# A hybrid decoder block on one core: unnormalised x + mixer split into three parts straight from its PSUM banks, and the RMS factor applied per expert place

## The chip, the cores and the metric

The kernel runs on 1 core of one Trainium2 chip. The metric is the device time of one execution in microseconds. Three runs of the kernel before gave 624.11, 624.51 and 628.24 us (median 624.51). The engines are called as the profile calls them: PE (matmul), PEld (PE's weight loads), DVE (vector), ACT (activation), POOL (GpSimd) and SP, which here only issues DMAs.

## The reference, cut to what matters

```python
# x: (1, 256, 1024) float32; 256 tokens, 1024 features; 4 groups x 8 experts, top 2 of one group per token
x = x + hybrid_mixer(rmsnorm(x, norm_mix_g), ...)          # mLSTM heads and S5 groups, then @ w_out
t = rmsnorm(x, norm_ffn_g)                                 # x * rsqrt(mean(x*x) + EPS) * g
g_logits = t @ rg_w + rg_b;  e_logits = t @ re_w + re_b    # choose a group, then two of its experts
for e in range(32):
    ye = (silu(t @ w_gate[e]) * (t @ w_up[e])) @ w_down[e]  # 1024 -> 512 -> 1024, all float32
    y = y + combine[:, e:e + 1] * ye
return rmsnorm(x + y, norm_final_g)
```

The 32 experts' weights are 192 blocks of 1 MiB, and each is read once.

## The kernel before, in words

**Tiling.** The 256 tokens are two blocks (b = 0, 1) of 128 partitions. The kernel has three stages. The mixer ends with `outs` (L797), which adds mixer @ w_out to x in four PSUM banks `WB` = 0, 1, 5, 7, one for each token block b and half q of the features. A prologue (L1015 to L1071) routes the tokens. A loop over 16 pairs of experts (L1083) follows, and then a tail.

**The prologue.** `residual` copies each bank to `x1` (a 1 MiB buffer, half 5). `squares` makes the sums from which POOL computes `r2`, the factor rsqrt(mean + EPS) of each token. `transpose1` and `logits` give the router's products. `choose` and `rank` are chains of small DVE instructions: which two experts a token takes (`msk`), and which of the 64 places of the expert it gets (`rk`). `rank` needs one small matmul (L899) between `choose` and its own DVE step (L901). `warm` is filler matmuls of the identity. `first` (L937) then writes a float32 one-hot matrix, times r2, and `gather_first` (L943) multiplies `x1` by it: the tokens of the first pair, sorted by place, in float32. `gains` (L950, DVE) multiplies by g2 into `xg`, the moving side of the expert products.

After the gather, DVE and ACT work out the mixing weights (`weights`, L909 to L917), and L1061/L1062 the largest number of tokens of an expert, in PSUM bank `UB` = 4. `parts_of_x` (L919) then makes x * r2 in a scratch buffer (half 22) and splits it into three bf16 parts `xp` whose sum is the float32 value. The gathers of all later pairs (L967) read these parts with bf16 one-hots `oh`: 48 matmuls, in pair 0 for pair 1 and in every odd pair up to 13 for the next two pairs.

**A pair.** The gate products (16 matmuls in bank `GB` = 2), Silu on ACT (L1096), the up products (16 in bank 4), act * up on DVE (L1103), four PE transposes (L1117), and the scatter operand: two transposes of the one-hot weights into columns 0 to 255 of bank 4 (L982), reduced and compared on DVE (L984, L985). Then comes the gather, if the pair has one, and the down products (16). All these matmuls are L994. The scatter of the pair before (L1009) lies between gate, up and transposes.

**What sets the order.** The schedule is manual: each engine runs its instructions in the order in which the program writes them, and the framework puts semaphore waits where two engines touch the same data. All PSUM work goes through one tile of eight banks.

**The weight queue.** `fetch(n)` issues the DMAs of the first n weight blocks, in order, on SP (L147). The blocks rotate through 23 buffers in the order `RO`; a DMA waits until its buffer's former user is done, and everything behind it on SP waits too. Blocks 21 and 22 (counted from 0) go into half 5, which is `x1`, and half 22, the scratch of `parts_of_x`. Block 23 reuses the buffer of block 0 and is free when half of pair 0's gate products are done.

Of the kernel before, what the change touches and what calls it, by code (L numbers as in the profile page):

```python
# [20 lines left out]
D = 1024  # L21
# [51 lines left out]
def tile_hymba(ctx, tc, x, norm_mix_g, w_in, conv_w, conv_b, i_bias, f_bias, mlstm_norm_g,  # L73
# [37 lines left out]
    oh = cuts(cst.bitcast(BF16), (2, 4, 64), start=2 * 1176)[0]  # L111
    ru = pool.tile([P, 2, 2, 8], U32, name="ru")
# [5 lines left out]
    RO = (14, 16, 18, 11, 10, 4, 19, 15, 7, 17, 20, 21, 12, 8, 1, 6, 0, 2, 3, 9, 13, 5, 22)  # L118
# [696 lines left out]
    fetch(14)  # L815
# [19 lines left out]
    fetch(16)  # L835
# [3 lines left out]
    fetch(18)  # L839
# [12 lines left out]
    def squares(b, q, e):  # L852
        cs = slice(512 * q, 512 * q + 512)
        if e is V:
            STT(sqs[:, cs], x1[:, b, cs], 1.0 / D, x1[:, b, cs], OP.mult, OP.mult, accum_out=sh[:, b, q:q + 1])
        else:
            ACT(sqs[:, cs], x1[:, b, cs], AF.Square, scale=1.0 / 32, accum_out=sh[:, b, q:q + 1])
# [39 lines left out]
    def rank(b):  # L897
# [5 lines left out]
        for e in range(2):  # L903
            first(b, e)
            yield
# [13 lines left out]
    def parts_of_x(b):  # L919

        t, r = xn[:, b], xp[:, :, b]
        ACT(t, x1[:, b], AF.Copy, scale=r2[:, b:b + 1])
        A.copy(r[:, 0], t)
        yield
        TT(t, t, r[:, 0], OP.subtract)
        A.copy(r[:, 1], t)
        yield
        TT(r[:, 2], t, r[:, 1], OP.subtract)

    xg, act, aT, ow, oh32 = cuts(mw, (8, 256), 512, (4, 128), (2, 2, 64), (2, 2, 64))
# [3 lines left out]
    def first(b, e):  # L936
        TS(oh32[:, b, e], places, rk[:, b, e:e + 1], r2[:, b:b + 1], OP.is_equal, OP.mult)  # L937

    def gather_first(q, bs=(0, 1)):
# [12 lines left out]
    def onehots(e0, es):  # L952

        for b in range(2):
# [80 lines left out]
    run(outs(7, 3, (1,), (1,)))  # L1035
    residual(1, 1)
# [3 lines left out]
    squares(1, 1, A)  # L1040
    warm(3, DN[0])
# [3 lines left out]
    run(rank0)  # L1045
    rank1, ch = rank(1), choose(1)
    next(ch)
    gather_first(0, (0,))
    gather_first(1, (0,))
    MM(PS[:, LB[1], 64:96], ones, msk[:, 0], start=True, stop=False, skip_group_check=True)  # L1050
    run(ch)
    warm(1, LB[0])
    next(rank1)
    warm(3, LB[0])
# [12 lines left out]
    for _ in range(3):  # L1067
        for g in pt:
            next(g, None)
    fetch(NP)  # L1070
# [12 lines left out]
    for pr in range(16):  # L1083
# [12 lines left out]
        ACT(act, PS[:, GB, :], AF.Silu)  # L1096
# [6 lines left out]
        TT(act, act, PS[:, UB, :], OP.mult)  # L1103
# [118 lines left out]
    with tc.If(most > PLACES):  # L1222
# [7 lines left out]
        with tc.For_i(0, 32, 1) as e:  # L1230
# [4 lines left out]
            for turn in range(2):  # L1235
# [3 lines left out]
                for q in range(2):  # L1239
                    for c in range(4):  # L1240
# [61 lines left out]
```

## Time and profile before

| what | value |
|---|---|
| time, three runs | 624.11, 624.51, 628.24 us |
| the profiled execution: its own time, its span | 628.37 us, 626.4 us |
| PE busy | 595.8 us (95%) |
| DVE, ACT, POOL busy | 218.1, 130.7, 57.9 us |
| chain that ended last | PE 56%, DMA 36%, DVE 3%, ACT 2% |
| expert products L994 | 1504 records, 338.8 us |
| DMA | 219.78 MB, mean 351 GB/s |

The profiled execution is one run of the program with the hardware profiler on. Its span runs from the first to the last instruction, and all times in rows count from the span's start. The chain that ended last is followed back from the end: where it names DMA, work waited for a block of weights. A float32 matmul shows as two records, so 48 records of L994 are 24 matmuls. The granted clock of PE is 1.00 at 2.4 GHz and 0.50 at 1.2 GHz.

### The profile page before, as it was taken

The page shows a single profiled execution, that of the slowest core. Times are in us where ns is not written, and L with a number is a line of the kernel's source. Part 1 is how long each engine was busy: PE and PEld are TensorE (multiplying, and loading weights), DVE is VectorE, ACT ScalarE, POOL GpSimd, SP SyncE. Part 2 cuts the span into 40 slices and gives each one's busy share as a digit, 9 for nine tenths or more (in the row PEclk, how much of TensorE's full clock was granted, in tenths as well). Part 3 has the DMA queues.
Part 4 walks back from the last instruction along what each step waited for, and adds up shares of the span by engine and source line. Part 5 has one row for each costly group of instructions (what it writes and reads, how often), then busy time and mean ns, then how long its engine had stood idle before and what let it go on. Part 6 is the DMA issues. An engine that isn't in the chain of part 4 may idle for free.

```text
span 626.4 us, 7955 instructions
## 1 busy us (share of the span) xinstructions
PE 595.8 (95%) x3176; PEld 321.8 (51%) x3176; DVE 218.1 (35%) x549; ACT 130.7 (21%) x234; POOL 57.9 (9%) x74
## 2 busy tenths in 40 slices
PE   8999997999999999999999999999998999899993
PEld 7787586788843533453353354335333534444242
DVE  5969951784462211131221212022120312121023
ACT  3481556521150010101101010010000010001023
POOL 7040228050000000000000000000000000000003
PEclk9999997999799999999999999999999999999997
DMA  8790149299569999999999999999999999999992
GB/s 227 260 313 13 46 170 389 98 387 390 201 225 419 422 419 419 420 420 420 420 418 421 417 422 418 419 420 420 420 419 419 421 420 419 420 418 422 417 332 79
DMA packets 51336, 219.78 MB, mean 351 GB/s; under 512 B 15236, under 2 KB 20448, under 8 KB 27232
## 3 DMA queue, kind: packets, MB, share of 16 engines
q1 hardware_dynamic: 50800, 218.17, 87.1%
q10 hardware_dynamic: 496, 1.06, 0.4%
q8 instruction: 27, 0.44, 0.3%
q14 instruction: 13, 0.11, 0.0%
HBM read 218.17 MB, written 1.05 MB: 350 GB/s over the span
## 4 chain that ended last, share of the span: by engine, by line
PE 56%; DMA 36%; DVE 3%; ACT 2%; issue 1%; POOL 1%; POOLq 0%; SPq 0%; DVEq 0%; ACTq 0%
PE psum L994 28%; DMA half<-in_expert_w_down_dram 13%; DMA half<-in_expert_w_up_dram 13%; DMA half<-in_expert_w_gate_dram 10%; PE psum L430 6%; PE psum L797 4%; PE psum L967 3%; PE psum L1009 2%; PE psum L438 2%; PE psum L943 1%; PE psum L1117 1%; DMA xs<-in_x_dram 1%; PE psum L449 1%; PE psum L1013 1%; PE psum L451 1%; PE psum L453 1%
## 5 line engine op out<-in xcount | busy, mean ns | idle before, releaser
L994 PE MATMUL psum<-half,mw 128*64 128x512 f32 x1504 | 338.8, 597 | 9.5 <-DMA half<-in_expert_w_up_dram 4.2
L994 PEld LDWEIGHTS psum<-half,mw 128*64 128x64 f32 x1504 | 110.0, 137 | 218.5 <-issue 187.1
L1001 DVE SCALAR_TENSOR_TENSOR Y<-psum,cst,Y 128x512 fp32r<-128x512 f32 x28 | 21.0, 751 | 134.2 <-ACT Y L1000 134.2
L1103 DVE TENSOR_TENSOR mw<-mw,psum 128x512 f32<-128x512 f32 x16 | 11.0, 688 | 143.7 <-PE psum L994 143.7
L1000 ACT ACTIVATE Y<-psum,cst 128x512 fp32r<-128x512 f32 x28 | 19.2, 688 | 191.2 <-PE psum L994 125.8
L430 PE MATMUL psum<-half,half 128*128 128x256 f32 x192 | 42.4, 380 | 0.4 <-DVE half L280 0.4
L967 PE MATMUL psum<-cst,xs 128*128 128x256 bf16 (+1 forms) x384 | 41.0, 267 | 0.0
L1140 POOL MEMSET mw<- 128x2 f32 x1 | 0.1, 99 | 436.0 <-PE psum L1117 436.0
L967 PEld LDWEIGHTS <-xs 128*128 128x128 bf16 x384 | 40.0, 144 | 0.0
L430 PEld LDWEIGHTS psum<-half,half 128*128 128x128 f32 x192 | 36.2, 190 | 5.7 <-DVE half L280 0.6
L1009 PE MATMUL psum<-Y,Sc 128*128 128x512 f32 x112 | 33.6, 422 | 0.0
L1118 ACT COPY mw<-psum 128x512 f32<-128x512 f32 x15 | 8.8, 587 | 113.9 <-PE psum L1117 113.8
L1009 PEld LDWEIGHTS psum<-Y,Sc 128*128 128x128 f32 x112 | 18.8, 188 | 25.2 <-issue 22.7
L420 POOL TENSOR_TENSOR half<-half,half 128x1024 fp32r<-128x1024 f32 x10 | 24.5, 2469 | 64.6 <-ACT half L419 46.8
L950 DVE TENSOR_TENSOR mw<-psum,cst 128x512 f32<-128x512 f32 x32 | 22.1, 692 | 22.1 <-PE psum L967 18.4
L797 PE MATMUL psum<-half,half 128*128 128x512 f32 x96 | 24.2, 402 | 0.3 <-ACT half L825 0.3
L1096 ACT ACTIVATE mw<-psum 128x512 f32<-128x512 f32 x16 | 9.6, 597 | 53.4 <-PE psum L994 53.4
L797 PEld LDWEIGHTS psum<-half,half 128*128 128x128 f32 x96 | 17.5, 188 | 4.6 <-ACT half L825 0.5
L984 DVE TENSOR_REDUCE cst<-psum 128x1 f32<-128x256 f32 x16 | 6.8, 425 | 27.1 <-PE psum L982 27.1
L975 DVE TENSOR_SCALAR mw<-cst 128x64 f32<-128x64 f32 x64 | 15.6, 308 | 0.0
L438 PE MATMUL psum<-half,half 128*128 128x512 f32 x32 | 14.2, 596 | 1.5 <-DVE half L598 1.5
L1117 PE MATMUL psum<-ident,mw 128*128 128x128 f32 x64 | 10.7, 290 | 1.7 <-DVE mw L1103 1.7
(344 smaller groups left out, 514.8 us busy)
## 6 DMA issues: line engine op xcount, KB each, us to landing
half<-in_expert_w_gate_dram SPq DMA_DIRECT2D x64, 1024.0 KB, 19.9
half<-in_expert_w_up_dram SPq DMA_DIRECT2D x64, 1024.0 KB, 19.9
half<-in_expert_w_down_dram SPq DMA_DIRECT2D x60, 1024.0 KB, 19.9
half<-in_w_in_dram SPq DMA_DIRECT2D x8, 1024.0 KB, 7.6
half<-in_w_out_dram SPq DMA_DIRECT2D x4, 1024.0 KB, 8.5
half<-in_expert_w_down_dram SPq DMA_DIRECT2D x6, 512.0 KB, 13.7
half<-in_w_in_dram SPq DMA_DIRECT2D x4, 512.0 KB
half<-in_expert_w_down_dram SPq DMA_DIRECT2D x4, 256.0 KB, 6.2
```

Source lines behind the costliest of these rows:

```text
L420: es[i].tensor_tensor(rests[i], w, made[i].bitcast(F32), OP.subtract)
L430: MM(PS[:, bk + m // 2, 256 * (m % 2):256 * (m % 2) + 256], w[:, at:at + 128], flat(h32, c), start=c == 0 and m % 2 == 0, stop=c == 7, ski ...
L438: MM(PS[:, bks[b], :], h32[:, c, b], raw[g, c // 2][:, 512 * (c % 2):512 * (c % 2) + 512], start=c == 0, stop=c == 7, skip_group_check=True)
L797: MM(PS[:, WB[2 * b + i], :], m[:, k % 4, ts], w[:, 512 * i:512 * i + 512], start=False, stop=n == 7 and m is ml, skip_group_check=True)
L950: TT(xg[:, cs, ss], PS[:, bk, :].rearrange("p (c s) -> p c s", c=n), fr(g2[:, cs], (1, n), (0, m)), OP.mult)
L967: MM(PS[:, DN[f % 2], m * c:m * c + m], xp[:, k, b, n * f + c::8], oh[:, b].rearrange("p e s -> p (e s)")[:, ss], start=c == b == k == 0, ...
L975: TS(ow[:, b, e], places, rk[:, b, 2 * pr + e:2 * pr + e + 1], wt[:, b, 2 * pr + e:2 * pr + e + 1], OP.is_equal, OP.mult)
L994: MM(PS[64 * e:64 * e + 64, bk, 0:w[e].shape[-1]], lhs[:, c, 64 * e:64 * e + 64], w[e], start=c == 0, stop=c == n - 1, skip_group_check=True)
L1000: ACT(hi, src, AF.Copy, scale=w)
L1001: STT(lo, src, w, hi.bitcast(F32), OP.mult, OP.subtract)
L1009: MM(PS[:, WB[2 * b + n], :], Sc[:, b], Y[:, k], start=False, stop=False, skip_group_check=True)
L1117: TR(PS[:, GB, 128 * c:128 * c + 128], act[:, c::4], ident)
```

## The change

The three bf16 parts are now made from the PSUM banks themselves, before the norm: `parts_of_x(b, q)` casts a bank to bf16 on ACT, subtracts on DVE, casts, and subtracts again, four times for a quarter of the data, and this stands among `residual`, `squares`, `choose` and `rank`. The first pair is gathered from these parts with bf16 one-hots. The factor r2, which is no longer in the data, is split into three bf16 parts (`parts_of_factors`), gathered by place with two matmuls of 3 columns for each pair (`factors`, into columns 256 to 263 of bank 4), and summed on DVE into `rp`. Silu takes `rp` as its scale, and act * up becomes act * (up * rp). No scratch buffer is needed, so half 22 moves forward in `RO` to the place behind half 8, the fetch calls reach one block further, and the last block (now in half 5, `x1`) is fetched once the transposes and squares have read `x1`.

```diff
-    RO = (14, 16, 18, 11, 10, 4, 19, 15, 7, 17, 20, 21, 12, 8, 1, 6, 0, 2, 3, 9, 13, 5, 22)
+    RO = (14, 16, 18, 11, 10, 4, 19, 15, 7, 17, 20, 21, 12, 8, 22, 1, 6, 0, 2, 3, 9, 13, 5)
...
-    fetch(14)
+    fetch(15)
...
-        for e in range(2):
-            first(b, e)
-            yield
+        onehots(0, (0, 1), (b,))
+        yield
...
+    def parts_of_x(b, q):
+        cs, t = slice(512 * q, 512 * q + 512), sqs[:, 512 * q:512 * q + 512]
+        r, src = xp[:, :, b, cs], PS[:, WB[2 * b + q], :]
+        A.copy(r[:, 0], src)
+        yield
+        TT(t, src, r[:, 0], OP.subtract)
+        yield
         A.copy(r[:, 1], t)
         yield
         TT(r[:, 2], t, r[:, 1], OP.subtract)
+        yield
+    def parts_of_factors():
+        V.tensor_copy(rpt[:, :, 0], r2)
+        TT(rtmp, r2, rpt[:, :, 0], OP.subtract)
+        V.tensor_copy(rpt[:, :, 1], rtmp)
+        TT(rpt[:, :, 2], rtmp, rpt[:, :, 1], OP.subtract)
...
-            for b in bs:
-                MM(PS[:, DN[q], 128 * c:128 * c + 128], x1[:, b, 4 * q + c::8],
-                   oh32[:, b].rearrange("p e s -> p (e s)"), start=c == b == 0, stop=b == 1, skip_group_check=True)
+            for k in range(3):
+                MM(PS[:, DN[q], 128 * c:128 * c + 128], xp[:, k, b, 4 * q + c::8],
+                   oh[:, b, 0:2].rearrange("p e s -> p (e s)"), start=c == b == k == 0, stop=b == 1 and k == 2,
+                   skip_group_check=True)
...
+    def factors(js):
+        for j in js:
+            at = PS[:, UB, 256 + 4 * j:259 + 4 * j]
+            for b in range(2):
+                MM(at, oh[:, b, 2 * j:2 * j + 2].rearrange("p e s -> p (e s)"), rpt[:, b], start=b == 0, stop=b == 1,
+                   skip_group_check=True)
+            V.tensor_reduce(rp[:, j:j + 1], at, AX.X, OP.add)
...
     for q in range(2):
-        gather_first(q, (1,))
+        gather_first(q, 1)
+    parts_of_factors()
     for b in range(2):
         weights(b)
     for b in range(2):
-        MM(PS[:, UB, 0:32], ones, msk[:, b], start=b == 0, stop=b == 1)
+        MM(PS[:, UB, 0:32], ones, msk[:, b], start=b == 0, stop=b == 1, skip_group_check=True)
     V.tensor_reduce(cnt[:, 0:1], PS[:, UB, 0:32], AX.X, OP.max)
     V.tensor_copy(cnti[:, 0:1], cnt[:, 0:1])
-    fetch(NP - 2)
-    xn = cuts(half(22), (2, 1024))[0]
-    pt = [parts_of_x(b) for b in range(2)]
-    for _ in range(3):
-        for g in pt:
-            next(g, None)
-    fetch(NP)
+    factors((0,))
     onehots(0, (2, 3))
...
-        ACT(act, PS[:, GB, :], AF.Silu)
+        ACT(act, PS[:, GB, :], AF.Silu, scale=rp[:, pr % 2:pr % 2 + 1])
...
-        TT(act, act, PS[:, UB, :], OP.mult)
+        STT(act, PS[:, UB, :], rp[:, pr % 2:pr % 2 + 1], act, OP.mult, OP.mult)
...
         if pr == 0:
+            factors((1,))
             gather((2, 3))
         elif pr % 2 and pr < 14:
+            factors((0, 1))
             gather(range(4))
```

The order of the instructions at three places follows (a row's brackets name the engine or DMA queue whose semaphore it waits for); line numbers are each kernel's own (the expert products are L994 before and L1011 after, the later gathers L967 and L984, `gains` L950 and L967).

PE, from the last matmuls of the first pair's gather to the loop's first product, before:

```order
L895 MATMUL psum<-ident 128x128 x3
L943 MATMUL psum<-mw,half_70_1132 128x128 [waits DVE_49]
L943 MATMUL psum<-mw,half_70_1132 128x128 x7
L1061 MATMUL psum<-cst 128x32 x2
L994 MATMUL psum<-half_35_665,mw 64x512 [waits DMAHW2_49,DVE_49]
```

and now:

```order
L950 MATMUL psum<-cst,xs 128x128
L1099 MATMUL psum<-cst 128x32 x2
L961 LDWEIGHTS cst
L961 MATMUL psum<-cst 128x3 [waits DVE_49]
L961 LDWEIGHTS cst
L961 MATMUL psum<-cst 128x3
L1011 MATMUL psum<-half_35_665,mw 64x512 [waits DMAHW2_49]
```

The gather is 24 bf16 matmuls for a token block in place of 8 float32 ones, and two factor matmuls with a wait for DVE now stand ahead of the first expert product.

DVE, at the same place, before:

```order
L950 TENSOR_TENSOR mw<-psum,cst 128x4x128 [waits PE_49,Activation_49]
L909 TENSOR_SCALAR cst<-cst 128x4
...
L917 SCALAR_TENSOR_TENSOR cst<-cst 128x32 [waits DVE_49]
L1062 TENSOR_REDUCE cst<-psum 128x1 [waits PE_49]
L1063 CAST cnti<-cst 128x1 [waits DVE_49]
```

and now:

```order
L967 TENSOR_TENSOR mw<-psum,cst 128x4x128 [waits PE_49]
L935 CAST cst<-cst 128x2
L936 TENSOR_TENSOR cst<-cst 128x2 [waits DVE_49]
L937 CAST cst<-cst 128x2 [waits DVE_49]
L938 TENSOR_TENSOR cst<-cst 128x2 [waits DVE_49]
L911 TENSOR_SCALAR cst<-cst 128x4
...
L919 SCALAR_TENSOR_TENSOR cst<-cst 128x32 [waits DVE_49]
L1100 TENSOR_REDUCE cst<-psum 128x1 [waits PE_49]
L1101 CAST cnti<-cst 128x1 [waits DVE_49]
L963 TENSOR_REDUCE cst<-psum 128x1 [waits PE_49]
```

L935 to L938 split r2; between them and L1100, the reduce that reads columns 0 to 31 of bank 4, stand the fourteen instructions of `weights` (L911 to L919, twice), as they stood behind `gains` before.

PE, in an odd pair, from the transposes to the gather, before:

```order
L1009 MATMUL psum<-Y,Sc 128x512 x2
L1117 MATMUL psum<-ident,mw 128x128 [waits DVE_49]
L1117 MATMUL psum<-ident,mw 128x128 x3
L982 MATMUL psum<-ident,mw 128x128 x2
L967 LDWEIGHTS xs
L967 MATMUL psum<-cst,xs 128x256
```

and now:

```order
L999 MATMUL psum<-ident,mw 128x128 x2
L961 LDWEIGHTS cst
L961 MATMUL psum<-cst 128x3 [waits DVE_49]
L961 LDWEIGHTS cst
L961 MATMUL psum<-cst 128x3
L961 LDWEIGHTS cst
L961 MATMUL psum<-cst 128x3 [waits DVE_49]
L961 LDWEIGHTS cst
L961 MATMUL psum<-cst 128x3
L984 LDWEIGHTS xs
L984 MATMUL psum<-cst,xs 128x256
```

Four matmuls and two waits for DVE stand between the scatter operand's transposes (L999, L982 before) and a gather that waited for nothing.

## Rows read from the trace of the kernel before

**Rows 1.** Timeline of PE, gathers of four odd pairs, one late wait: start, length.
```profile
212.22 5.40 PE L967 MATMUL psum<-cst,xs 128*128 128x256 bf16 x48
...
265.75 5.40 PE L967 MATMUL psum<-cst,xs 128*128 128x256 bf16 x48
...
426.37 5.40 PE L967 MATMUL psum<-cst,xs 128*128 128x256 bf16 x48
...
540.14 3.65 PE L994 MATMUL psum<-half,mw 128*64 128x512 f32 x14 [1.33 <-DMA half<-in_expert_w_up_dram]
...
545.45 5.40 PE L967 MATMUL psum<-cst,xs 128*128 128x256 bf16 x48
```

**Rows 2.** Stretches: length, PE busy (records), granted clock, DMA share, GB/s.
```profile
163.00:176.40 13.40, 13.40 (x65) 0.82 0.14 59
176.40:183.20 6.80, 6.80 (x34) 1.00 0.71 220
...
190.00:426.00 236.00, 234.17 (x1173) 1.00 1.01 419
```

**Rows 3.** Waits of SP, 85 to 200 us: total, times, longest.
```profile
SPq L147 <- PE psum L943: 12.5, 1, 12.5
...
SPq L147 <- ACT half L922: 6.2, 1, 6.2
SPq L147 <- DVE xs L928: 4.3, 1, 4.3
```

**Rows 4.** Timeline of PE in the prologue, and the loop's start.
```profile
158.98 4.20 PE L943 MATMUL psum<-mw,half 128*128 128x128 f32 x16
...
163.83 0.47 PE L899 MATMUL psum<-cst 128*128 128x32 f32 x2
...
165.54 3.90 PE L943 MATMUL psum<-mw,half 128*128 128x128 f32 x16
...
169.73 13.95 PE L994 MATMUL psum<-half,mw 128*64 128x512 f32 x64
```

**Rows 5.** Timeline of DVE in the prologue; in brackets idle before it, and its end.
```profile
151.56 0.69 DVE L850 COPY half<-psum 128x512 f32<-128x512 f32 x1 [0.39 <-PE psum L797]
...
164.34 0.19 DVE L901 SCALAR_TENSOR_TENSOR cst<-psum,cst 128x32 f32<-128x32 f32 x1 [2.74 <-PE psum L899]
...
169.54 0.69 DVE L950 TENSOR_TENSOR mw<-psum,cst 128x512 f32<-128x512 f32 x1 [1.19 <-PE psum L943]
...
173.58 0.18 DVE L1062 TENSOR_REDUCE cst<-psum 128x1 f32<-128x32 f32 x1
```

**Rows 6.** Groups by line and shape, 130 to 215 us: busy us, mean ns, idle before.
```profile
L928 DVE TENSOR_TENSOR xs<-half,xs 128x1024 bf16<-128x1024 f32 x2 | 2.4, 1222 | 0.0
```

**Rows 7.** Timeline of PE, the 128-column bf16 gather in pair 0.
```profile
185.38 3.13 PE L967 MATMUL psum<-cst,xs 128*128 128x128 bf16 x48
```

**Rows 8.** Timeline, pair 1: the scatter operand on PE and DVE beside the gather.
```profile
212.00 0.38 PE L982 MATMUL psum<-ident,mw 128*128 128x128 f32 x2
...
212.42 0.42 DVE L984 TENSOR_REDUCE cst<-psum 128x1 f32<-128x256 f32 x1 [1.06 <-PE psum L982]
212.76 0.42 DVE L985 TENSOR_SCALAR Sc<-psum 128x256 fp32r<-128x256 f32 x1
213.73 0.69 DVE L950 TENSOR_TENSOR mw<-psum,cst 128x512 f32<-128x512 f32 x1 [0.55 <-PE psum L967]
```

**Rows 9.** Timeline of PE: 24 expert products at full clock, and behind a clock drop.
```profile
550.78 10.52 PE L994 MATMUL psum<-half,mw 128*64 128x512 f32 x48
...
578.19 11.87 PE L994 MATMUL psum<-half,mw 128*64 128x512 f32 x48 [0.38 <-ACT mw L1118]
```

**Rows 10.** Stretches of 2 us, columns as in the second group: the clock's falls and rises.
```profile
160.00:162.00 2.00, 2.00 (x9) 0.78 1.00 422
...
166.00:168.00 2.00, 2.00 (x10) 0.52 0.05 20
...
576.00:578.00 2.00, 1.80 (x14) 0.88 0.99 410
...
580.00:582.00 2.00, 2.00 (x10) 0.77 1.02 422
```

More of the change, by code (lines that the diff above doesn't have):

```diff
@@ L111, in tile_hymba @@
     oh = cuts(cst.bitcast(BF16), (2, 4, 64), start=2 * 1176)[0]
+    rpt = cuts(cst.bitcast(BF16), (2, 3), start=2 * 1496)[0]
+    rtmp, rp = cuts(cst, 2, 2, start=1500)
     ru = pool.tile([P, 2, 2, 8], U32, name="ru")
     cnti = pool.tile([P, 8], I32, name="cnti")
-    RO = (14, 16, 18, 11, 10, 4, 19, 15, 7, 17, 20, 21, 12, 8, 1, 6, 0, 2, 3, 9, 13, 5, 22)
+    RO = (14, 16, 18, 11, 10, 4, 19, 15, 7, 17, 20, 21, 12, 8, 22, 1, 6, 0, 2, 3, 9, 13, 5)
     NP = len(RO)
@@ L854, in squares @@
         if e is V:
-            STT(sqs[:, cs], x1[:, b, cs], 1.0 / D, x1[:, b, cs], OP.mult, OP.mult, accum_out=sh[:, b, q:q + 1])
+            STT(junk1, x1[:, b, cs], 1.0 / D, x1[:, b, cs], OP.mult, OP.mult, accum_out=sh[:, b, q:q + 1])
         else:
-            ACT(sqs[:, cs], x1[:, b, cs], AF.Square, scale=1.0 / 32, accum_out=sh[:, b, q:q + 1])
+            ACT(junk1, x1[:, b, cs], AF.Square, scale=1.0 / 32, accum_out=sh[:, b, q:q + 1])
         if q:
@@ L950, in gains, with onehots @@
         TT(xg[:, cs, ss], PS[:, bk, :].rearrange("p (c s) -> p c s", c=n), fr(g2[:, cs], (1, n), (0, m)), OP.mult)
-    def onehots(e0, es):
-        for b in range(2):
+    def onehots(e0, es, bs=(0, 1)):
+        for b in bs:
             for e in es:
@@ L1013, in scatter1 @@
             MM(to, S1[:, pr - 14, b], y[:, cs], start=start and y is yh, stop=stop and y is yl, skip_group_check=True)
+    part = {(b, q): parts_of_x(b, q) for b in range(2) for q in range(2)}
+    sqs, junk1 = cuts(mw, 1024, 512, start=2048)
     residual(0, 0)
+    next(part[0, 0])
     squares(0, 0, V)
+    next(part[0, 0])
+    next(part[0, 0])
     for n in range(6, 8):
@@ L1025, in tile_hymba @@
     transpose1(0, 1)
+    next(part[0, 1])
     residual(1, 0)
+    next(part[0, 0])
+    next(part[0, 1])
+    next(part[0, 1])
     run(outs(6, 2, (1,), (1,)))
@@ L1029, in tile_hymba @@
     squares(1, 0, A)
+    next(part[1, 0])
+    next(part[0, 1])
     for q in range(2):
@@ L1035, in tile_hymba @@
     run(outs(7, 3, (1,), (1,)))
+    fetch(NP - 1)
     residual(1, 1)
@@ L1040, in tile_hymba @@
     squares(1, 1, A)
+    fetch(NP)
+    next(part[1, 0])
+    next(part[1, 0])
+    next(part[1, 1])
     warm(3, DN[0])
@@ L1045, in tile_hymba @@
     run(rank0)
+    next(part[1, 1])
+    next(part[1, 1])
     rank1, ch = rank(1), choose(1)
     next(ch)
-    gather_first(0, (0,))
-    gather_first(1, (0,))
+    next(part[1, 0])
+    next(part[1, 1])
+    for q in range(2):
+        gather_first(q, 0)
     MM(PS[:, LB[1], 64:96], ones, msk[:, 0], start=True, stop=False, skip_group_check=True)
     run(ch)
-    warm(1, LB[0])
+    warm(4, LB[0])
     next(rank1)
-    warm(3, LB[0])
+    warm(4, LB[0])
     run(rank1)
     for q in range(2):
-        gather_first(q, (1,))
+        gather_first(q, 1)
+    parts_of_factors()
     for b in range(2):
@@ L1246, in tile_hymba @@
                        fr(g2[:, 4 * q:4 * q + 4], (1, 4), (0, 128)), OP.mult)
+                for b in range(2):
+                    MM(PS[:, 4, 256:259], o1[:, b], rpt[:, b], start=b == 0, stop=b == 1)
+                V.tensor_reduce(rp[:, 0:1], PS[:, 4, 256:259], AX.X, OP.add)
                 for bk, w in ((2, wgt), (3, wup)):
@@ L1249, in tile_hymba @@
                         MM(PS[:, bk, :], xo[:, c], w[c // 4][:, c % 4], start=c == 0, stop=c == 7)
-                ACT(ao, PS[:, 2, :], AF.Silu)
-                TT(ao, ao, PS[:, 3, :], OP.mult)
+                ACT(ao, PS[:, 2, :], AF.Silu, scale=rp[:, 0:1])
+                STT(ao, PS[:, 3, :], rp[:, 0:1], ao, OP.mult, OP.mult)
                 for c in range(4):
```

17 lines of the change are left out of this document (5 added, 12 removed).

## The prediction

> **What bounds the kernel now.** I read the chain that ended last first (PE 56%, DMA 36%), then PE's timeline for the distance between equal points of the loop, then the DMA's rate by stretch, then the waits of SP, and last the prologue on PE and DVE. The gathers of odd pairs are equal points two pairs apart. From 212.22 to 265.75 is 53.53 us, and from 212.22 to 426.37 is four times that, to 0.03: up to there PE never waits for weights. From 426.37 to 545.45 is 119.08, 12.0 more than two times 53.53: here PE waits for blocks, as the 1.33 before 540.14 shows [rows 1]. So the loop is bound by PE until about 426, by the DMA until 540.14, and by PE after that; only 12.0 us are the DMA's. The DMA itself runs at 419 GB/s, a block in 2.5 us, from about 183 on; before that it stands nearly still from 163 to 176.4 (59 GB/s) and at half rate to 183.2 [rows 2]. The reason is on SP: block 21 waits 12.5 us for the first gather's reads of x1 and 6.2 for ACT's, block 22 another 4.3 for the scratch, and all others stand behind them [rows 3].
>
> **What the change does to the weights.** Both waits go: half 22 is free with half 8, and x1 after its squares near 159. Blocks 0 to 22 are then in before the loop begins, and the queue runs on once half of pair 0's gate products (3.5 us of the 13.95 for gate and up, [rows 4]) is done. With the loop's start that I find below (173.9, and a slow first stretch of 1.35), that is 178.8; I allow 1 us until data moves, which is 3.4 us ahead of the full rate at 183.2. Of blocks 21 and 22, 1.5 of 2.1 MB had moved by then (220 GB/s for 6.8 us, [rows 2]); the rest is 1.4 us. So blocks land about 4.8 us earlier. The block that PE had to wait for at 540.14 lands at 535.3; by the terms below PE wants it at 545. The waits for weights are gone: **-12.0**. More than this the earlier loads cannot give.
>
> **The loop's start.** Three things change ahead of it.
> First, the splitting. It adds to DVE four subtractions from a bank, as long as a copy of a bank (0.69, [rows 5]), and four in SBUF of half the shape of L928's 1.22, so 0.61 [rows 6]: 5.2 us. ACT gets eight casts, of which the ones ahead of x1T's copies delay the logits by 0.3 to 0.4. Placing them in the new order, I get the end of choose(1) 2.8 us later. DVE waited 2.74 us there for PE [rows 5], since PE was behind with the float32 gather (4.20, [rows 4]); that gather is now 24 matmuls of 65 ns (3.13 / 48, [rows 7]), 1.6 us. So rank(1)'s matmul stays within +0.4 of its place; one more warming matmul behind it, two records of about 0.24 as L943's at that clock (3.90 / 16), adds 0.5. The cover is used up: what else is put on DVE here would count in full.
> Second, the gather of block 1: 24 matmuls in place of 3.90 us. It takes 1.6 at 2.4 GHz and twice that at 1.2, at which PE ran from 161.1 to 167.9 (0.78 and 0.52 of a stretch, [rows 10]); I take 2.3. It ends at 169.4 + 0.4 + 0.5 - 1.6 = 168.7, between 167.6 and 169.9.
> Third, the factor matmuls, L961. They need only r2's parts and the one-hots, but the count that they wait for in the built program is that of L1100, the last DVE instruction that reads bank 4. Ahead of it on DVE stand gains (0.1 and 0.69), four small instructions (0.18 each as L1062, 0.7) and both weights with their exponentials on ACT: 170.23, the end of L950, to 173.76, the end of L1062, is 3.53 [rows 5]. With 0.2 for the hand-over and two matmuls of 65 ns, the loop begins 5.2 after the gather, at 173.9 instead of 169.73: **+4.2**, between 3.1 and 5.4.
>
> The trace of before has no matmul that waits for another column of its bank. The Trainium skill, "PSUM — Partial Sum Buffer", section "PSUM bank collisions raise a hardware error", has the rule that software guards PSUM by bank and quadrant, "not by address", since engines that touch the same bank collide even in different columns. By that rule the wait stands and costs the 4.2; by addresses it would end with L938, 3.5 us earlier. No run here shows a collision; the counts in the program agree with the rule.
>
> **The clock at the start.** PE now has almost nothing to do for 5 us before its first expert product. The nearest stall is at 577: after small matmuls and transposes the clock fell to 1.2 GHz, at 577.5, and came back at 580.9 [rows 10], and the next 24 products took 11.87 instead of 10.52 [rows 9]. I take the same here, **+1.35**; nothing if the clock holds, twice that if it comes back later.
>
> **The odd pairs.** PE's order puts the factors behind the scatter operand's transposes L982, whose result in columns 0 to 255 of bank 4 DVE reads twice. The first L961 waits for the second of these reads. Before, the gather began at 212.22 and L985 ended at 213.18 [rows 8]; with 0.07 to hand over that is 1.03. Two matmuls take 0.13. The second couple writes the same bank and waits for the first couple's sum on DVE: 0.2 from the last matmul of a group to DVE's start (twelve of the gather's 48 end at 213.53, L950 starts at 213.73, [rows 1, 8]), 0.18 for the sum, 0.06 back: 0.43. Then 0.13. Together 1.7 us, all on PE's path, since nothing else stands between. Seven odd pairs (1 to 13): **+11.9**, with 1.3 and 2.1 as ends, 9.1 to 14.7. Pair 0 has one couple: **+1.2**.
>
> **The rest.** Act * up with three operands on DVE lies under the scatter's four matmuls except in pairs 0 and 15; Silu's scale lies under the up products; the sums into rp lie under the gather's first bank. I give them **+0.1**; without that cover each would cost its own length. Tail and mixer are as they were.
>
> **The sum.** -12.0 + 4.2 + 1.35 + 11.9 + 1.2 + 0.1 = +6.75, against the profiled execution's own time, 628.37: 635.1. All low ends give +1.0, all high ends +12.8. The profiled execution is 3.9 above the median of the runs and beside the slowest of them. If these 3.9 us are waits for weights, they go in any case, and the changed kernel is at 635.1 in every run; if they lie elsewhere, its median is 624.51 + 6.75 = 631.3. One trace does not tell, so I take the middle: **633 us**.
>
> **Rivals.**
> *The waits cost little.* If the factor matmuls were held by their own inputs alone, the loop would begin at 168.7 + 0.1 + 0.69 + 0.7 + 0.2 = 170.4 (+0.7), the clock would cost half (0.7), and the 30 factor matmuls 65 ns each (2.0). The blocks then come 9.0 earlier and meet PE's need at about 531, so the 12.0 still go: -12.0 + 0.7 + 0.7 + 2.0 + 0.1 = -8.5, 616 to 620 us, faster. For it: the columns are disjoint and the change frees 12.0 us that are really waited for. Against it: both waits stand in the order, and PE has nothing else to do in them. It decides if a stall in an odd pair is under 0.6 us.
> *The clock falls in odd pairs too.* After the scatter PE has transposes, 1.03 of waiting, four tiny matmuls and 0.43 of waiting: some 2.5 us of little work, like the 2.7 before 577.5. If each of seven cost 1.35 [rows 9], 9.5 more: 641 to 645 us. Against it: the gather behind it is dense, and at 577 matmuls of eight rows filled 2 us. The Trainium skill, "TensorE: Matmul & The Clock Gate", section "A second HAM failure mode: psum-queue depth-cycling", describes such a loss from short idles between groups of matmuls; this trace has stalls of 1.33 us before 540.14 with the clock at 1.00 around them, which speaks against it.
> *A draw.* The low ends together (start +3.1, clock 0, pairs 9.1 and 0.8): 625.5 to 629.4, no change to be seen.
>
> **How the numbers follow.** Forecast 0.70, waits that cost little 0.08, falling clock 0.10, draw 0.12. The range, 626 to 640, holds the forecast with its two readings of the 3.9 us and most of its bounds and part of the draw; it leaves out the first rival, most of the second, and thin ends, 0.2 in all. A change of 1%, about what a measurement of this kernel can tell, is 618.3 or 630.8. The first rival is faster; the draw and one part in seven of the forecast are within 1%; the rest is slower: 0.08, 0.22, 0.70.
>
> **What would show it.** Gathers of odd pairs 53.53 + 1.7 = 55.2 us apart from the first to the last, with no wait for DMA before L1011; DMA at full rate by 180 and blocks waiting for buffers, not PE for blocks; PE idle some 5 us before the first L1011, released by L1100; idle of about 1 us before L961 in odd pairs, released by L1002; 0.50 in the clock at the loop's start. I am wrong if the loop starts before 172, if the gathers are under 54.5 apart, or if PE still waits for blocks near 540.

## Result and the profile after

| | before | after |
|---|---|---|
| median of the runs | 626.06 us (8 runs, 624.11 to 628.64) | 631.61 us (8 runs, 628.89 to 633.47) |
| profiled execution: its time, its span | 628.37, 626.4 us | 633.47, 631.8 us |
| chain that ended last | PE 56%, DMA 36% | PE 90%, DMA 1% |

The changed kernel is 0.8% slower: the ratio of the times is 1.0079, interval 1.005 to 1.0109. The forecast was 633 us. More runs of the kernel before, taken beside the experiments, moved its median to 626.6. Two executions, one of e3_both below (873.94 us at a mean clock of 0.65) and one of the kernel before (770.52 us at 0.75), are far slower than all others and stand in no comparison.

**The waits for weights are gone.** First the chain that ended last, by engine, then the waits of PE in the changed kernel (total us, times, longest).

```profile
PE 90%; DVE 4%; ACT 2%; issue 1%; DMA 1%; POOL 0%; POOLq 0%; DVEq 0%; ACTq 0%
```

And the waits:

```profile
PE psum L961 <- DVE Sc L1002: 6.8, 8, 0.8
PE psum L961 <- DVE cst L1100: 4.6, 1, 4.6
...
PE psum L961 <- DVE cst L963: 1.8, 7, 0.3
```

No product L1011 waits for a DMA any more; three waits of the new factor matmuls L961 stand there instead, 13.2 us in all. On the weight queue SP now waits for buffers that PE has to free, 141.1 us in 40 waits where it was 15.5 us before. That wait, and then two stretches of its timeline (start, length of a group of issues):

```profile
SPq L150 <- PE psum L1011: 141.1, 40, 18.9
```

```profile
157.72 22.01 SPq L150 DMA_DIRECT2D half<-in_expert_w_down_dram  x4
179.81 6.77 SPq L150 DMA_DIRECT2D half<-in_expert_w_gate_dram  x4
...
529.45 8.14 SPq L150 DMA_DIRECT2D half<-in_expert_w_gate_dram  x4
```

The waits of 12.5, 6.2 and 4.3 us for x1 and the scratch [rows 3] are gone, and 1.3 us for the squares' reads of x1 is what is left of them. The group that begins at 157.72 ends when the first buffer comes free, and the queue runs on at 179.81 (178.8 was forecast). The four gate blocks issued from 529.45 on were issued from 532.69 on before; here is that row of the kernel before.

```profile
532.69 7.80 SPq L147 DMA_DIRECT2D half<-in_expert_w_gate_dram  x4
```

So blocks come 3.2 us earlier from the span's start, and 5.0 earlier from the end of the mixer, which came 1.72 later in this execution (see the account). The one that PE waited for at 540.14 [rows 1] would land at 536.9, and PE wants it 5.31 before the gather [rows 1], less the 1.66 that the pair now waits in between: 552.46 - 1.66 - 5.31 = 545.5 (the gather's row is below). It has 8.6 us to spare.

**The loop's start and the odd pairs.** The timeline of PE after, in two answers: the start of the loop, then two odd pairs and two later places.

```profile
172.97 0.19 PE L961 MATMUL psum<-cst 128*128 128x3 bf16 x2 [4.55 <-DVE cst L1100]
173.09 16.57 PE L1011 MATMUL psum<-half,mw 128*64 128x512 f32 x64
...
192.44 0.19 PE L961 MATMUL psum<-cst 128*128 128x3 bf16 x2 [0.84 <-DVE Sc L1002]
192.49 3.18 PE L984 MATMUL psum<-cst,xs 128*128 128x128 bf16 x48
```

```profile
220.46 0.19 PE L961 MATMUL psum<-cst 128*128 128x3 bf16 x2 [0.84 <-DVE Sc L1002]
220.90 0.19 PE L961 MATMUL psum<-cst 128*128 128x3 bf16 x2 [0.25 <-DVE cst L963]
220.95 5.44 PE L984 MATMUL psum<-cst,xs 128*128 128x256 bf16 x48
...
276.14 5.44 PE L984 MATMUL psum<-cst,xs 128*128 128x256 bf16 x48
...
552.46 5.44 PE L984 MATMUL psum<-cst,xs 128*128 128x256 bf16 x48
...
584.39 12.22 PE L1011 MATMUL psum<-half,mw 128*64 128x512 f32 x48 [0.46 <-ACT mw L1150]
```

The gathers stand 55.19 us apart where they stood 53.53 apart [rows 1], from the first to the last: (552.46 - 220.95) / 6 = 55.25, the excess over 55.19 being 0.34 us in pair 12. The first 64 records of the loop take 16.57 where they took 13.95 [rows 4].

Stretches after: length, PE, PEld, DVE, ACT and POOL busy (records), granted clock, DMA share, GB/s.

```profile
166.00:170.60 4.60, 2.42 (x33) 2.32 (x32) 2.92 (x14) 0.39 (x3) 0.00 (x0) 1.00 0.96 397
...
173.00:180.00 7.00, 7.00 (x22) 2.17 (x23) 1.80 (x10) 0.00 (x0) 0.00 (x0) 0.61 0.00 0
184.00:624.00 440.00, 423.77 (x2214) 184.55 (x2210) 99.40 (x253) 47.70 (x84) 5.06 (x9) 1.00 0.98 401
```

The clock is 0.61 in the loop's first 7 us, after 4.55 us in which PE had nothing to do, and 1.00 over the pairs, but for 584 to 588 (0.65 and 0.50), the place of the drop before [rows 9]. In the DMA's column the pause of the weights is the second row (nothing from 173 to 180). The last row's 401 GB/s takes in the end, where the loads are over; over the stretch of [rows 2], in the columns given there, the rate is what it was before (419):

```profile
190.00:426.00 236.00, 228.31 (x1190) 1.00 1.01 418
```

So the DMA is as busy as before, and what is new is that PE does not wait for it.

**The account**, span against span (+5.4): waits for weights -13.9 (12.0 between 426.37 and 545.45, and 1.9 in product groups after that, 11.37 and 9.80 us long where they are now 10.52 and 8.74); odd pairs 7 x 1.66 = +11.6, and 0.34; pair 0 +1.05; the loop's start +3.36; its first 64 records +2.6; the slow stretch at 584 +0.35, 12.22 for 11.87 [rows 9]. That is +5.4. Of the start's +3.36, 1.72 is not the change's: the mixer, which is the same in both kernels, ended that much later in this execution. The first `residual` is the mark for it:

```profile
150.11 0.69 DVE L853 COPY half<-psum 128x512 f32<-128x512 f32 x1 [5.49 <-PE psum L800]
```

The same instruction started at 148.39 before. The clock in the mixer was 0.61 from 44 to 50 us and 0.54 from 50 to 56 after, and 1.00 in both stretches before; it fell so in one of the ten experiments' profiles too (the first one of the two mendings together), and not in the others, so it comes and goes with the execution. In the eight other profiles of kernels that are edits of the changed one, where the clock did not fall there, the mark lies between 145.78 and 147.53, ahead of the 148.39 of before. From that mark to the first L1011 it is 22.98 after and 21.34 before.

### The profile page after: what moved, and what is told of

Same layout as the page of the kernel before. It is cut to its first block, busy times and chain, and to the rows that moved or that the text cites. A ratio compares the mean times of both kernels' runs of the same rounds, so it can differ in the third digit from the quotient of the medians.

```text
span 631.8 us, 8097 instructions
## 1 busy us (share of the span) xinstructions
PE 593.0 (94%) x3232; PEld 316.6 (50%) x3232; DVE 222.7 (35%) x573; ACT 130.2 (21%) x236; POOL 57.7 (9%) x74
## 3 DMA queue, kind: packets, MB, share of 16 engines
HBM read 218.17 MB, written 1.05 MB: 347 GB/s over the span
## 4 chain that ended last, share of the span: by engine, by line
PE 90%; DVE 4%; ACT 2%; issue 1%; DMA 1%; POOL 0%; POOLq 0%; DVEq 0%; ACTq 0%
PE psum L1011 54%; PE psum L433 7%; PE psum L984 6%; PE psum L1026 5%; PE psum L800 3%; PE psum L441 2%; PE psum L1149 2%; PE psum L524 1%; PE psum L522 1%; DMA xs<-in_x_dram 1%; ACT mw L1150 1%; PE psum L1030 1%; PE psum L452 1%; PE psum L650 1%; PE psum L454 1%
## 5 line engine op out<-in xcount | busy, mean ns | idle before, releaser
L1011 PE MATMUL psum<-half,mw 128*64 128x512 f32 x1504 | 334.1, 601 | 3.2 <-ACT mw L1150 3.2
L1011 PEld LDWEIGHTS psum<-half,mw 128*64 128x64 f32 x1504 | 105.4, 138 | 212.0 <-issue 198.2
L1135 DVE SCALAR_TENSOR_TENSOR mw<-psum,cst,mw 128x512 f32<-128x512 f32 x16 | 12.0, 750 | 148.5 <-PE psum L1011 148.5
L984 PE MATMUL psum<-cst,xs 128*128 128x256 bf16 (+1 forms) x384 | 41.3, 267 | 0.0
L984 PEld LDWEIGHTS <-xs 128*128 128x128 bf16 x384 | 39.7, 145 | 0.0
L967 DVE TENSOR_TENSOR mw<-psum,cst 128x512 f32<-128x512 f32 x32 | 22.1, 691 | 24.8 <-PE psum L984 23.7
L1128 ACT ACTIVATE mw<-psum,cst 128x512 f32<-128x512 f32 x16 | 11.0, 687 | 53.2 <-PE psum L1011 53.2
L1001 DVE TENSOR_REDUCE cst<-psum 128x1 f32<-128x256 f32 x16 | 6.8, 424 | 27.4 <-PE psum L999 27.4
L961 PE MATMUL psum<-cst 128*128 128x3 bf16 x32 | 3.0, 164 | 13.1 <-DVE Sc L1002 6.8
L441 PE MATMUL psum<-half,half 128*128 128x512 f32 x32 | 13.9, 593 | 0.0
```

The lines of the kernel that those rows point to most:

```text
L441: MM(PS[:, bks[b], :], h32[:, c, b], raw[g, c // 2][:, 512 * (c % 2):512 * (c % 2) + 512], start=c == 0, stop=c == 7, skip_group_check=True)
L967: TT(xg[:, cs, ss], PS[:, bk, :].rearrange("p (c s) -> p c s", c=n), fr(g2[:, cs], (1, n), (0, m)), OP.mult)
L984: MM(PS[:, DN[f % 2], m * c:m * c + m], xp[:, k, b, n * f + c::8], oh[:, b].rearrange("p e s -> p (e s)")[:, ss], start=c == b == k == 0, ...
L1011: MM(PS[64 * e:64 * e + 64, bk, 0:w[e].shape[-1]], lhs[:, c, 64 * e:64 * e + 64], w[e], start=c == 0, stop=c == n - 1, skip_group_check=True)
```

## Experiments

The theory: the earlier blocks took 12 to 14 us of waiting away, and the three waits of L961 gave more than that back, all of them because its result lies in a PSUM bank that DVE has still to read: other columns of it, or the sum of the product before. The rival theories were that the waits come from the work itself (matmuls and sums, their inputs, their latency), and that the earlier blocks brought nothing. The medians, with the ratio to the kernel before (626.5 to 626.7) and its 95% interval:

| run | what | us | ratio |
|---|---|---|---|
| e1_odd | odd pairs mended by order | 622.05 | 0.9925 (0.9899 to 0.9951) |
| e2_start | loop's start mended by order | 624.57 | 0.9957 (0.9932 to 0.9981) |
| e3_both, e3_again | both | 614.84, 615.03 | 0.9806 (0.977 to 0.9843), 0.9824 (0.9801 to 0.9847) |
| e4_late | the change, two blocks held back | 635.33 | 1.0127 (1.0088 to 1.0166) |
| e5_both_late | both mended, two blocks held back | 626.85 | 1.0018 (0.9999 to 1.0037) |
| e6_before_waits | before, with the pairs' waits of L961 | 626.59 | 1.0014 (0.9993 to 1.0036) |
| e7_bank | the change, factors in bank 6 | 621.09 | 0.9936 (0.9912 to 0.9961) |
| e8_warm | the change, fillers ahead of the loop | 628.60 | 1.0034 (1.0013 to 1.0055) |
| e9_bank_two | bank 6, both products ahead of one sum | 617.06 | 0.9852 (0.983 to 0.9875) |

**Odd pairs by order (e1_odd).** The factor products go behind the scatter operand's transposes, ahead of DVE's reads, and one sum serves both.

```diff
     def scatter_operand(pr, js=()):
         ...
             TR(PS[:, bk, 128 * b:128 * b + 128], ow[:, b].rearrange("p e s -> p (e s)"), ident)
+        factor_products(js)
         ...
         TS(Sc if pr < 14 else S1[:, pr - 14], src, 0.0, None, OP.not_equal)
+        if js:
+            factor_sums(js)
```

> The changed kernel, with the factor matmuls of odd pairs and pair 0 right behind the scatter operand's transposes and ahead of DVE's reads of bank 4, both couples summed by one reduce; the prologue is the changed one. Theory (the two waits on bank 4 in a pair cost 1.4 of the 1.66 us that a gather-to-gather distance grew per odd pair): gathers 53.8 apart instead of 55.2, PE's path 10.8 us shorter, 621 to 622 us, DMA landing just as PE wants its blocks near pair 13. Rival (the late start of the loop and its slow clock hold the loss, and the pairs are paced by the weights anyway): gathers still about 55 apart, 630 to 632 us.

Its timeline of PE (L990 is the gather):

```profile
215.74 5.44 PE L990 MATMUL psum<-cst,xs 128*128 128x256 bf16 x48
269.54 5.44 PE L990 MATMUL psum<-cst,xs 128*128 128x256 bf16 x48
```

The gathers are 53.80 apart: of the 1.66 us a pair 0.27 is left, and the other 1.39 was waiting. 622.05 us is 9.6 less than the change, and these waits alone are 7 x 1.39 = 9.7.

**The start by order (e2_start).** The parts of r2 are made ahead of the last gather, the factor product and its sum ahead of the mixing weights.

```diff
     run(rank1)
+    parts_of_factors()
     for q in range(2):
         gather_first(q, 1)
-    parts_of_factors()
-    for b in range(2):
-        weights(b)
     ...
+    factor_products((0,))
     V.tensor_reduce(cnt[:, 0:1], PS[:, UB, 0:32], AX.X, OP.max)
     V.tensor_copy(cnti[:, 0:1], cnt[:, 0:1])
-    factors((0,))
+    factor_sums((0,))
+    for b in range(2):
+        weights(b)
```

> The changed kernel, with r2's parts made ahead of the last gather and the factor matmul and its sum ahead of the mixing weights, so that the first expert product waits for gains alone; the odd pairs are the changed ones. Theory: the loop starts 0.9 us after the gather instead of 5.1, PE stays at 2.4 GHz (the first 64 records take 13.9 us and not 16.6), so 4.2 + 2.6 us less, about 625 us, that is level with the kernel before. Rival (the stall is hidden, since the weights' arrival sets the pace later): 630 to 632 us.

Its timeline of PE at the start:

```profile
166.96 0.20 PE L959 MATMUL psum<-cst 128*128 128x3 bf16 x2
167.08 13.95 PE L1017 MATMUL psum<-half,mw 128*64 128x512 f32 x64
```

The loop begins 19.79 after the first residual, in place of 22.98, and its first 64 records take 13.95: -3.2 and -2.6. The gathers stay 55.20 apart. The median fell by 7.0, 1.2 more than these two; single executions differ by more than that.

**Both (e3_both, e3_again).**

> Both mendings together. Theory: the two losses add, 10.8 + 6.8 us off 631.6, and since blocks also land some 7 us earlier, PE and DMA meet: 614 to 616 us, 1.6 to 2% under the kernel before. Rival (the DMA is the bound as soon as PE is faster, as it was before from 426 us on): 620 us or more, with waits for weights of 5 us and more in pairs 10 to 13.

> The kernel with the factor products grouped ahead of DVE's reads and the start mended, once more and beside the version above, since one of its runs had taken 873.94 us. Expected: 614 to 616 us as in its other runs, and no more than 1 us from the version above, if both only take the waits away; if one of them has a cost of its own (the sum in two steps, a start that is 0.8 us later), 1 to 2 us between them.

Timeline of e3_both:

```profile
211.06 5.44 PE L990 MATMUL psum<-cst,xs 128*128 128x256 bf16 x48
...
480.03 5.44 PE L990 MATMUL psum<-cst,xs 128*128 128x256 bf16 x48
...
534.62 5.44 PE L990 MATMUL psum<-cst,xs 128*128 128x256 bf16 x48
```

Five times 53.79 to the sixth gather, then 54.59: the up products of pair 13 take 11.35 in place of 10.52 with the clock at 1.00. The DMA runs at 418 to 430 GB/s there, so these are probably short waits for a block within the group, by place and size; the view of waits does not name them, and this is argued and not shown. With both mended the kernel is 1.8 to 1.9% faster than before: this is what the earlier blocks are worth, as e5_both_late below shows.

**The blocks held back in the change (e4_late).** The old order of buffers, the fetch calls as they were before, and blocks 21 and 22 wait for small ACT copies behind pair 0's Silu.

```diff
-    RO = (14, 16, 18, 11, 10, 4, 19, 15, 7, 17, 20, 21, 12, 8, 22, 1, 6, 0, 2, 3, 9, 13, 5)
+    RO = (14, 16, 18, 11, 10, 4, 19, 15, 7, 17, 20, 21, 12, 8, 1, 6, 0, 2, 3, 9, 13, 5, 22)
     ...
         ACT(act, PS[:, GB, :], AF.Silu, scale=rp[:, pr % 2:pr % 2 + 1])
+        if pr == 0:
+            A.copy(half(22)[:, 0:512], act)
+            A.copy(x1[:, 0, 0:512], act)
+            fetch(NP + 4)
```

> The changed kernel with the old buffer order and the last two blocks held back: halves 5 and 22 are touched by small copies on ACT behind pair 0's Silu, and the queue goes on only then. Blocks then land some 8.7 us later. Theory (the changed kernel is held by PE alone, with about 8.6 us to spare at the block that was critical before): 631 to 633 us, the same as with early blocks. Rival (the early blocks are what keeps the changed kernel from being slower still): 637 to 640 us.

SP and PE of this run:

```profile
155.67 30.25 SPq L150 DMA_DIRECT2D half<-in_expert_w_down_dram  x4
186.02 2.39 SPq L150 DMA_DIRECT2D half<-in_expert_w_gate_dram  x4
```

```profile
495.45 5.44 PE L984 MATMUL psum<-cst,xs 128*128 128x256 bf16 x48
546.83 3.65 PE L1011 MATMUL psum<-half,mw 128*64 128x512 f32 x14 [1.33 <-DMA half<-in_expert_w_up_dram]
553.70 5.44 PE L984 MATMUL psum<-cst,xs 128*128 128x256 bf16 x48
```

The last gap is 58.25, 3.05 over 55.20, and the median is 3.7 above the change's. The block that PE waits for lands at 546.83, 399.3 after the first residual (147.53 here); in the change it would land at 536.9, 386.8 after it. So the delay is 12.5 us and not the 8.7 that I had reckoned with. PE gets to this place 1.1 later than in the change (its loop begins 1.5 later after the mark, at 172.05, and the first 64 records take 0.4 less), so with 8.6 us to spare it should wait 2.8; it waits 3.05. The median lies between the two forecasts, 2.3 above the theory's and 1.7 below the rival's: the time to spare was there, but the blocks came later than I had said.

**The blocks held back in the mended kernel (e5_both_late).** The edits of e3_both and e4_late together.

> The kernel with the factor products grouped ahead of DVE's reads and the start mended (the experiment that gave 614.8 us), and with the two expert blocks that the change has loading early held back behind the Silu of pair 0, by some 11 to 12 us, as in the experiment that gave 635.3 us. Theory (the early loads are worth what they bring only where TensorE is not late by itself): all of the delay is paid as waits for weights in the odd pairs from the fifth on, 614.8 + 9 to 12 = 624 to 627 us. Rival (the transfers have slack, or catch up): 615 to 618 us.

Its waits of PE:

```profile
PE psum L1020 <- DMA half<-in_expert_w_up_dram: 4.2, 4, 1.3
...
PE psum L1020 <- DMA half<-in_expert_w_gate_dram: 2.1, 2, 1.1
```

626.85 us, 11.8 to 12.0 above the mended kernel, with PE waiting for blocks in the same places and sizes as before. Counted from the first residual of each run, the gate blocks that were issued from 532.69 on before go out at 532.21 - 147.41 = 384.8 here, at 517.43 - 145.78 = 371.7 in e3_again and at 532.69 - 148.39 = 384.3 before. So the blocks are some 13 us later than in the mended kernel and as late as before, and the time is that of the kernel before too. So much the same delay costs 3.7 us where PE is late by itself, and 12 where it is not.

**The waits alone in the kernel before (e6_before_waits).** It makes factor products of three columns of x (their sums are not used) in bank 4, at the change's place, in pair 0 and the odd pairs; the product ahead of the loop and its wait are not in it.

```diff
+    def spare(js):
+        for j in js:
+            at = PS[:, UB, 256 + 4 * j:259 + 4 * j]
+            for b in range(2):
+                MM(at, oh[:, b, 2 * j:2 * j + 2].rearrange("p e s -> p (e s)"), xp[:, 0, b, 0:3], ...)
+            V.tensor_reduce(cst[:, 1502 + j:1503 + j], at, AX.X, OP.add)
     ...
         elif pr % 2 and pr < 14:
+            spare((0, 1))
             gather(range(4))
```

> The kernel before with the waits alone: in pair 0 and in the seven odd pairs it also makes the factor products (of bfloat16 columns of x, the sums are not used) in bank 4 at the place where the changed kernel makes them, and their two sums on DVE. The gathers then stand 55.2 us apart (53.5 in the kernel before). Theory (the kernel before has about 12 us in which TensorE waits for weights after 426, so that TensorE's delays are taken out of that wait and the changed kernel's gain is only seen where both are gone): 627 to 629 us, the waits for weights shrink from 13.9 us to 2 or less. Rival (the delays come on top, since the loads are paced by the buffers that TensorE gives back): 626.6 + 7 x 1.66 + 1.05 = 639 us.

Its timeline of PE:

```profile
212.28 0.19 PE L991 MATMUL psum<-xs,cst 128*128 128x3 bf16 x2 [0.85 <-DVE Sc L985]
212.72 0.19 PE L991 MATMUL psum<-xs,cst 128*128 128x3 bf16 x2 [0.25 <-DVE cst L993]
212.77 5.44 PE L967 MATMUL psum<-cst,xs 128*128 128x256 bf16 x48
...
488.16 5.44 PE L967 MATMUL psum<-cst,xs 128*128 128x256 bf16 x48
...
538.02 3.65 PE L1002 MATMUL psum<-half,mw 128*64 128x512 f32 x14 [0.54 <-DMA half<-in_expert_w_up_dram]
...
544.84 5.44 PE L967 MATMUL psum<-cst,xs 128*128 128x256 bf16 x48
```

The same two waits, the gathers 55.08 apart (five times from 212.77 to 488.16), and a last gap of 56.68: 1.6 us of waiting for weights where the kernel before has 12.0. The time is that of the kernel before, to 0.4%: some 12 us of new waits on PE cost nothing where PE was waiting for the DMA anyway.

**Another bank (e7_bank).** Same instructions, same order.

```diff
-            at = PS[:, UB, 256 + 4 * j:259 + 4 * j]
+            at = PS[:, DN[1], 4 * j:4 * j + 3]
```

> The changed kernel with one edit: the factor products go to columns 0 to 7 of bank 6 (DN[1]) in place of columns 256 to 263 of bank 4; same instructions in the same order. Theory (TensorE waits because DVE has columns 0 to 255 of the same bank still to read): the waits of 0.84 and 0.25 us go from every odd pair, the gathers stand 53.8 us apart in place of 55.2, pair 0 loses its 1 us, the loop starts about 3.4 us earlier (it then waits for the second gain, the four small parts and one product alone), its first 64 records take 13.95 us and not 16.56; about 1 us of waiting for weights comes back near pair 13. 631.6 - 9.7 - 1.0 - 3.4 - 2.6 + 0.7 = 615 to 617 us. Rival (the added products and sums themselves, or their latency, make the time, wherever they are put): 630 to 632 us and gathers 55.2 apart. Between them (only the first reader's wait goes, the product then waits for its own inputs): about 623.

Its timeline of PE at the start and in pair 1, then DVE beside pair 1:

```profile
166.19 0.19 PE L961 MATMUL psum<-cst 128*128 128x3 bf16 x2 [1.04 <-DVE cst L938]
166.31 13.95 PE L1011 MATMUL psum<-half,mw 128*64 128x512 f32 x64
...
182.03 0.19 PE L961 MATMUL psum<-cst 128*128 128x3 bf16 x2
```

```profile
209.03 0.19 PE L961 MATMUL psum<-cst 128*128 128x3 bf16 x2
210.11 0.19 PE L961 MATMUL psum<-cst 128*128 128x3 bf16 x2 [0.89 <-DVE cst L963]
210.16 5.44 PE L984 MATMUL psum<-cst,xs 128*128 128x256 bf16 x48
```

```profile
209.57 0.41 DVE L1002 TENSOR_SCALAR Sc<-psum 128x256 fp32r<-128x256 f32 x1
209.90 0.15 DVE L963 TENSOR_REDUCE cst<-psum 128x1 f32<-128x3 f32 x1
```

This is the clearest of the runs: by the bank's number alone the first product waits for L938, its own input, in place of L1100, and in the pairs for nothing; the loop begins 19.45 after the first residual. What I had not seen is the second product: it shares bank 6 with the first, whose sum stands on DVE behind the reads L1001 and L1002, so 0.89 of the 1.09 us comes back and the gathers stand 54.8 apart. Hence 621.09, between the two times expected.

**Bank 6, both products ahead of one sum (e9_bank_two).**

```diff
+        at = PS[:, DN[1], 0:8].rearrange("p (j k) -> p j k", k=4)[:, :, 0:3]
         for j in js:
-            at = PS[:, UB, 256 + 4 * j:259 + 4 * j]
             for b in range(2):
-                MM(at, ...)
-            V.tensor_reduce(rp[:, j:j + 1], at, AX.X, OP.add)
+                MM(at[:, j], ...)
+        V.tensor_reduce(rp[:, js[0]:js[-1] + 1], at[:, js[0]:js[-1] + 1], AX.X, OP.add)
```

> The changed kernel with the factor products in bank 6, as in the experiment that gave 621.1 us, and in the odd pairs both products ahead of one sum for both. Theory (the 0.88 us that was left in every odd pair is the second product waiting until DVE, behind its reads of bank 4, has summed the first, which lies in the same bank 6): the wait goes, the gathers stand 53.8 us apart in place of 54.8, TensorE runs up to the transfers and waits some 1 to 2 us for weights near pair 13: 621.1 - 7 x 1.0 + 1 = 614 to 616 us, as with the products grouped ahead of DVE's reads. Rival (the second product waited for the one-hots or for something else that comes that late): 54.8 apart, 621 us.

Its timeline of PE in pair 1 and the gather of pair 3:

```profile
211.11 0.24 PE L960 MATMUL psum<-cst 128*128 128x3 bf16 x4
211.21 5.44 PE L983 MATMUL psum<-cst,xs 128*128 128x256 bf16 x48
...
265.01 5.45 PE L983 MATMUL psum<-cst,xs 128*128 128x256 bf16 x48
```

The four factor matmuls run without a wait and the gathers are 53.80 apart, so the second product had waited for the first's sum. 617.06 is 1.1 above the range expected and 2.0 above e3_again. The wait of 1.04 for L938 that is left at its start may be half of that; this is not shown, and the two intervals overlap. This one function, rewritten, turns 0.8% slower into 1.5% faster; the order of e3_both gives 1.8 to 1.9%.

**The clock at the start (e8_warm).** Fillers in the wait; the start does not move.

```diff
     V.tensor_copy(cnti[:, 0:1], cnt[:, 0:1])
+    warm(14, LB[0])
     factors((0,))
```

> The changed kernel with 14 more products of the identity with itself on TensorE (about 4 us, their result is not used) ahead of the first factor product, inside the 4.55 us in which TensorE waits for DVE before the loop. The loop cannot start earlier by it. Theory (the 2.6 us by which the first 64 records of the loop are longer than before come from the clock that falls in that wait): first 64 records 13.95 us, the clock 1.00 from 168 to 180, in all 2.6 us less than the changed kernel: about 629 us. Rival (the clock was lost for another reason, by the gathers ahead of it or by the start of the block loads): 16.5 us for the 64 records, no change, 631.6 us. If the fillers run at the lower clock they take 8 us and the start comes 3 to 4 us later: 635 us.

Its timeline of PE:

```profile
165.22 3.37 PE L898 MATMUL psum<-ident 128*128 128x128 f32 x28
169.95 0.19 PE L961 MATMUL psum<-cst 128*128 128x3 bf16 x2 [1.36 <-DVE cst L1100]
170.07 13.95 PE L1011 MATMUL psum<-half,mw 128*64 128x512 f32 x64
```

The loop begins 23.00 after the first residual (22.98 in the change), the 64 records take 13.95, the clock is 1.00 from 165 to 180. The median is 3.0 lower than the change's, 2.6 of it this row. So the clock was lost in that wait, and the idle of 1.36 that is left did not lose it.

## Why the prediction was right, and where its terms were off

The mechanism held: what the DMA gives back is spent by L961's waits for a bank, and the sum comes out slower. 633 was forecast, 631.61 measured.

- **The weights**, -12.0 forecast, -13.9 measured. I had counted the late blocks up to 545.45 and not the 1.9 us inside the product groups behind it. The blocks come 5.0 earlier from the first residual (4.8 forecast; 3.2 from the span's start). But the term is no property of the loads: e4_late and e5_both_late price much the same delay at 3.7 and at 12 us, and e6_before_waits prices the pairs' waits at nothing in the kernel before. What can be added up is the longer of two paths, PE's and the DMA's. The sum was right because after the change only PE's was left.
- **The loop's start**, +4.2 forecast, +1.64 measured from the first residual (+3.36 from the span's start, 1.72 of it the mixer's). The step that was wrong is the gather's end at 168.7, which is 20.3 after the first residual; it came 17.9 after. I had kept PE's place in the old prologue, where the clock had fallen from 161.1 to 167.9 [rows 10], for the new one, where it stayed at 1.00. That is 1.5 of the 2.4: in e4_late, at 0.50 from 164 to 166, the same gather took 2.39 (2.3 forecast) and ended 19.4 after the mark. The other 0.9 is mostly rank(1)'s matmul, 15.0 after the mark in both, where I had 15.8 (the old place and 0.4). Against my own sign, a loop that starts before 172, the 173.09 stands only by the mixer's 1.72. e6_before_waits, with the old prologue at full clock, begins its loop 20.48 after the mark, so that part of the old 21.34 was that execution's. The wait for L1100 itself, gather's end to loop, was 5.1 of the 5.2 forecast.
- **The clock at the start**, +1.35 forecast, +2.6 measured: the upper of the two bounds. The stall that I priced it by [rows 9] had small matmuls in it; in this one PE had nothing to do, and the clock stayed at 0.50 until 178.
- **The odd pairs**, 1.7 forecast, 1.66 measured, released by L1002 and L963 as forecast. The Trainium skill, "PSUM — Partial Sum Buffer", section "PSUM bank collisions raise a hardware error", has the guard go by bank and quadrant (32 of the partitions) and not by address; e7_bank agrees, where the bank's number alone took the first wait from 4.55 to 1.04 us at the start and from 0.84 to nothing in the pairs. **Pair 0**, 1.2 forecast, 1.05 measured: its gather begins 1.86 after its transposes began, and 0.81 before. The rest, +0.1: 0.34 in pair 12 and 0.35 at 584.
- **The baseline.** 624.51 was a low median of three runs; by 626.6 the slowdown is 5.0 us and not the 8.5 that 633 meant, and so it lies at 0.8%, just inside the 1% for which I had given 0.22, and not over it, for which I had given 0.70. That 633 came within 1.4 us is luck in part: the change was forecast 3.5 too large, and the median it was added to was 2.1 too low. Of the 3.9 us that I could not place these 2.1 are one part. The rest lies ahead of the loop and is not a wait for weights: e6_before_waits, the same code up to there, has its first residual 1.18 earlier (147.21) and its loop another 0.86 earlier. The profiled execution after is 1.9 above its median as well, at the lowest clock of its eight runs (0.976, while the fastest had 0.987).
- **The rivals.** Waits that cost little: e9_bank_two is that kernel, at 617.06, inside the 616 to 620 given; the change is not it, since both waits stand. The falling clock in odd pairs: it is 1.00 in a stretch of 10 us around the wait in each of the seven. The draw: the pairs cost 11.6 where it had 9.1, and the clock 2.6 where it had nothing.

## What to carry to other kernels

A small result put into free columns of a PSUM bank waited here for DVE's earlier reads of other columns of that bank, with all that stood ahead of them in DVE's queue: give such a result a bank whose reader is done, or write it before the reads are issued, and sum what shares the bank in one instruction. A gain in waits for DMA and a loss on PE do not add; work out both paths and take the longer, and where a change loses, look whether the loss only covers the gain. Measure a start from the end of the stage ahead of it, not from the beginning of the span.

## What I had not expected of the hardware

The clock's falls are not fixed to a place in the program: the mixer had 0.54 to 0.61 from 44 to 56 us in two of the profiles and 1.00 in the others, and around the last gather it was 1.00 in the changed kernel and 0.50 from 164 to 166 in e2_start and e4_late, which have nearly the same instructions there. The first residual, the mark of the mixer's end, lay between 145.78 (e3_again) and 150.11 (the changed kernel), though nothing ahead of it differs among these kernels but the time at which some blocks are asked for. Three profiles have an idle of 4.55 to 4.57 us on PE and none of them kept the clock behind it: 16.17 to 16.57 us for the first products (e4_late, e1_odd, the changed kernel) in place of 13.95. Idles of 1.04 to 1.36 us cost none.
